# RWKV-7 mixer of a decoder trunk: the second half of a pair done for both heads at a time, with K = 64 products alternating between row groups

## The chip, the cores and the metric

The kernel runs on one core of one Trainium2 chip. The metric is the device time of one execution in microseconds, taken as the median of several runs. Engines are named as in the profile: PE (TensorE), PEld (its weight loads), DVE (VectorE), ACT (ScalarE), POOL (GpSimd), SP (SyncE, which issues the DMAs).

## The reference

Two decoder layers work on 512 tokens of width 1024. Each layer normalizes x, projects it by one matrix w_in, runs four token mixers (MLA, HGRN2, S5, RWKV-7) on slices of the projection, merges them with gates, and then does cross attention and a gated FFN. The change is inside RWKV-7, which has 8 heads of 64 channels. Per head and token:

```
def step(st, inp):
    r_t, k_t, v_t, w_t, kk_t, a_t = inp
    sa = jnp.einsum('bhvk,bhk->bhv', st, -kk_t)
    st = (st * w_t[:, :, None, :] + sa[..., None] * (kk_t * a_t)[:, :, None, :]
          + v_t[..., None] * k_t[:, :, None, :])
    return st, jnp.einsum('bhvk,bhk->bhv', st, r_t)
```

## The kernel before, in words

Dense products (`dense`, lines 331 to 333) stand for nearly all of the kernel. Each 128x128 block of weights is split in two fp32r parts, and three 128x512 products a block are added up in a bank of tag mm.

RWKV is computed in chunks of 128 tokens, four of them. `rwkv_pair` handles two heads at a time: head 0 lies on partitions 0 to 63, head 1 on 64 to 127. There are four pairs a layer, eight in all. A pair has a front half on bank tag st (one bank): elementwise work that makes al, be, kt and rt, then the product be x al for each head (line 908, K = 64), masked into rab by a predicated copy (line 909), then the inverse of a triangular matrix by 31 short steps on DVE (lines 924 and 926) and small products. The back half uses bank tag rw (two banks, handed out in turn, so that a new one waits for the one two before it to be released) and tag rwy (one bank). It transposes al, be, kt and v (line 993). Then a loop over the two heads does the rest, head 0 first: three masked K = 64 products (line 1016, copies at 1017), gak x v (1020), U (1024), the output and state matrices RY and PQ (1035, 1036), and then four steps over the chunks, in each of which a y product (1047) goes into the bank of tag rwy and a state product (1050, 64 columns) is scaled by DVE (1051) for the next step. Behind the loop come the normalization of y, a transpose, and a gating product (1083) whose bank is the last one of tag rw in the pair.

In grb and grk each chunk has 256 columns: 64 for head 0, 128 for the head in hand (the masked product, written anew for each head), 64 for head 1. All these products are f32; each stands in the trace as two matmuls.

The order of the instructions on each engine is made when the program is built. A scheduler takes instructions by priority and by its own estimate of when operands and banks are free. Pairs have their place in the order of the input projections (`mixers`, `in_order`), and dense products of those projections are put in where a pair has to wait. At run time each engine takes its instructions in that order.

Of the kernel before, what the change touches and what calls it, by code (L numbers as in the profile page):

```python
# [9 lines left out]
F32 = mybir.dt.float32  # L10
# [4 lines left out]
ALU = mybir.AluOpType  # L15
# [5 lines left out]
S = 512  # L21
MEM = 256
P = 128
# [77 lines left out]
UPPER, UPPER_EQ, HGM = 0, 1, 2  # L101
# [151 lines left out]
class Trunk:  # L253
# [62 lines left out]
    def bank(self, tag="mm", bufs=None):  # L316
        bufs = BANKS[tag]
        return self.ps.tile([P, 512], F32, tag=tag, name=tag, bufs=bufs)
# [470 lines left out]
    def rwkv_consts(self, pool):  # L789

        nc = self.nc
        z = lambda n, shape: pool.tile(shape, F32, name=n)
        self.gak = z("rgak", [P, 4, P])
        self.grb, self.grk = (z(n, [P, 4, 2 * P]) for n in ("rgrb", "rgrk"))
        self.rab = z("rab", [P, 2, 4, P])
        self.rmt = z("rmt", [P, 8, P])
        self.rm64 = z("rm64", [P, 8, 64])
        self.rvz = [z(f"rvz{h}", [P, 4, P]) for h in range(2)]
        self.rsi = [[z(f"rsi{h}{i}", [P, 64]) for i in range(4)] for h in range(2)]
        for t in [self.gak, self.grb, self.grk, self.rmt, self.rm64] + self.rvz:  # L800
            nc.gpsimd.memset(t, 0.0)
        nc.vector.tensor_copy(self.rab, self.ident.unsqueeze(1).unsqueeze(1).to_broadcast([P, 2, 4, P]))
        for h in range(2):
            for t in self.rsi[h]:
                nc.vector.tensor_copy(t, self.kcm(f"eye_k{1 - h}"))
# [20 lines left out]
    def rwkv_pair(self, l, j, pool, hv):  # L826

        nc = self.nc
        V, G, AC, PE = nc.vector, nc.gpsimd, nc.scalar, nc.tensor
        vj = lambda n: self.v(l, n, j)  # L830
        hj = lambda n: self.half(l, n, j)
        tl = lambda n, shape=None, bufs=1: pool.tile(shape or [P, S], F32, tag=n, name=n, bufs=bufs)
        c3 = lambda t: t.rearrange("p (c f) -> p c f", c=4)
        w = lambda n, shape=None: pool.tile(shape or [P, S], F32, tag="rfront", name=n, bufs=2)
        bank = lambda: self.bank("st")
# [12 lines left out]
        if l:  # L848
            vf = w("rvf")
            self.dma(vf, self.r_d[0][2, j])  # L850
            ps = bank()
# [7 lines left out]
        ps = bank()  # L859
# [5 lines left out]
        ps = bank()  # L865
# [13 lines left out]
        ff = tl("rff", [P, 3], 2)  # L879
# [12 lines left out]
        ps = bank()  # L892
        for c in range(4):
            PE.matmul(ps[:, c * P:(c + 1) * P], rb[:, 2 * c:2 * c + 2].rearrange("p h f -> p (h f)"), self.ident,
                      start=True, stop=True)
        kk = w("rkk")
        V.scalar_tensor_tensor(out=kk, in0=k, scalar=vj("k_k"), in1=ps, op0=ALU.mult, op1=ALU.mult)
        al, be, kt, rt = tl("ral", bufs=NB), tl("rbe", bufs=NB), tl("rkt"), tl("rrt")
# [1 line left out]
        V.scalar_tensor_tensor(out=be, in0=a, scalar=1.0, in1=kk, op0=ALU.add, op1=ALU.mult)  # L900
        V.scalar_tensor_tensor(out=be, in0=be, scalar=-0.5, in1=e2, op0=ALU.mult, op1=ALU.mult)

        for h in range(2):
            r0 = slice(64 * h, 64 * h + 64)
            ps = bank()
            for c in range(4):
                cs = slice(c * P, (c + 1) * P)
                PE.matmul(ps[:, cs], be[r0, cs], al[r0, cs], start=True, stop=True)
            V.copy_predicated(out=self.rab[:, h], mask=self.mask(UPPER), data=c3(ps))
        dg = tl("rdg", [P, 32, 8, 4])  # L910
        rab8 = self.rab.rearrange("p h c t -> p (h c) t")
        for q in range(4):
# [9 lines left out]
        for t in range(1, 32):  # L922
            n = t // 4 + 1
            V.tensor_tensor(out=tmp[:, :n, :t + 1], in0=M[:, :t + 1, :n].rearrange("p s c -> p c s"),  # L924
                            in1=E[:, t, :t + 1].unsqueeze(1).to_broadcast([P, n, t + 1]), op=ALU.mult)
# [15 lines left out]
        ps = bank()  # L941
# [9 lines left out]
        ps = bank()  # L951
# [10 lines left out]
        ps = bank()  # L962
# [4 lines left out]
        ps = bank()  # L967
# [13 lines left out]
        bon = tl("rbon", [P, 8], 2)  # L981
        V.tensor_copy(bon, st[:, 0:8])

        w = lambda n, shape=None: pool.tile(shape or [P, S], F32, tag="rback", name=n, bufs=3)
        bank = lambda: self.bank("rw")
        rh2 = tl("rrh", [P, 2, 4, P])
        rh = [rh2[:, h] for h in range(2)]
        gak, grb, grk = self.gak, self.grb, self.grk

        def tposed(src):  # L990
            ps = bank()
            for c in range(4):
                PE.transpose(ps[:, c * P:(c + 1) * P], src[:, c * P:(c + 1) * P], self.ident)
            return c3(ps)

        ps = tposed(al)
# [1 line left out]
            hs = slice(64 * h, 64 * h + 64)  # L998
            AC.copy(out=rh[h][:, :, hs], in_=ps[:, :, hs])
        for gt, x in ((grb, be), (grk, kt)):  # L1000
            AC.copy(out=gt.rearrange("p c (b f) -> p c b f", b=4)[:, :, 0::3],
                    in_=tposed(x).rearrange("p c (b f) -> p c b f", b=2))
        ps = tposed(v)
        for h in range(2):
            AC.copy(out=self.rvz[h][:, :, 64 - 64 * h:P - 64 * h], in_=ps[:, :, 64 * h:64 * h + 64])
        py = self.bank("rwy")
        for h in range(2):
            r0 = slice(64 * h, 64 * h + 64)
            vs = slice(64 - 64 * h, P - 64 * h)
            vz = self.rvz[h]  # L1010
            for gt, x, y, m in ((gak, kt, al, UPPER), (grb[:, :, 64:192], be, rt, UPPER_EQ),
                                (grk[:, :, 64:192], kt, rt, UPPER_EQ)):
                ps = bank()
                for c in range(4):
                    cs = slice(c * P, (c + 1) * P)
                    PE.matmul(ps[:, cs], x[r0, cs], y[r0, cs], start=True, stop=True)  # L1016
                V.copy_predicated(out=gt, mask=self.mask(m), data=c3(ps))
            ps = bank()
            for c in range(4):
                PE.matmul(ps[:, c * 64:c * 64 + 64], gak[:, c], vz[:, c, vs], start=True, stop=True)  # L1020
            AC.copy(out=rh[h][:, :, vs], in_=ps[:, :256].rearrange("p (c f) -> p c f", c=4))
            ps = bank()
            for c in range(4):
                PE.matmul(ps[:, c * P:(c + 1) * P], MT[:, 4 * h + c], rh[h][:, c], start=True, stop=True)
            U = w("rU", [P, 4, P])
            AC.copy(out=U, in_=c3(ps))
            RY = w("rRY")
            PQ = tl("rPQ", [P, 3, 64], 2)
            yo, po = (64, 0) if h == 0 else (0, 128)
            for b in range(2):  # L1030
                ps = bank()
                for c in range(2 * b, 2 * b + 2):
                    g, o = ((64 * h, 64 * h + 192), 0) if c < 3 else ((64, 192), yo)
                    out = ps[:, 192 * (c % 2) + o:192 * (c % 2) + o + g[1] - g[0]]
                    PE.matmul(out, U[:, c], grb[:, c, g[0]:g[1]], start=True, stop=False)  # L1035
                    PE.matmul(out, vz[:, c], grk[:, c, g[0]:g[1]], start=False, stop=True)
                p3 = ps[:, :384].rearrange("p (c f) -> p c f", c=2)
                y = lambda t: c3(t)[:, 2 * b:2 * b + 2]
                V.tensor_tensor(out=y(RY)[r0], in0=p3[r0, :, yo:yo + P], in1=y(rt)[r0], op=ALU.add)
                AC.copy(out=y(RY)[vs], in_=p3[vs, :, yo:yo + P])  # L1040
                n = 2 - b
                V.tensor_tensor(out=PQ[:, 2 * b:2 * b + n], in0=p3[:, :n, po:po + 64],
                                in1=self.kcm(f"eye_k{h}").unsqueeze(1).to_broadcast([P, n, 64]), op=ALU.add)
            V.memset(self.rsi[h][0][r0], 0.0)
            for c in range(4):
                si = self.rsi[h][c]
                PE.matmul(py[:, c * P + 64 * h:c * P + 64 * h + 64], RY[:, c * P:(c + 1) * P], si, start=True, stop=True)
                if c < 3:
                    ps = bank()
                    PE.matmul(ps[r0, :64], PQ[:, c], si, start=True, stop=True)  # L1050
                    V.tensor_scalar(out=self.rsi[h][c + 1][r0], in0=ps[r0, :64], scalar1=ff[r0, c:c + 1], scalar2=None,
                                    op0=ALU.mult)

        y8 = py.rearrange("p (g f) -> p g f", g=8)
        mu = tl("rmu", [P, 8])
# [12 lines left out]
                        in1=lnw.unsqueeze(1).to_broadcast([P, 4, P]), op=ALU.mult)  # L1068
        b4 = bon.rearrange("p (c h) -> p c h", c=4)
        y4 = y2.rearrange("p (c h) f -> p c h f", c=4)  # L1070
        for h in range(2):
            vs = slice(64 - 64 * h, P - 64 * h)
            nc.vector.tensor_tensor(out=y4[:, :, h], in0=self.rvz[h][:, :, vs], in1=b4[:, :, h:h + 1].to_broadcast([P, 4, 64]),
                            op=ALU.mult)
        nc.vector.tensor_tensor(out=yc, in0=yc, in1=y2, op=ALU.add)
        ps = bank()
# [3 lines left out]
        ps = bank()  # L1080
# [557 lines left out]
```

## Time and profile before

| what | us |
|---|---|
| three runs | 2773.11, 2774.59, 2781.51 |
| median | 2774.59 |
| profiled execution | 2776.61 |
| its span | 2774.5 |
| PE busy in it | 2714.2 (98%) |
| DVE busy in it | 1816.6 (65%) |
| ACT busy in it | 1112.5 (40%) |

The mean granted clock of TensorE is 0.991. The span runs from the first to the last instruction. Busy times of matmuls overlap and their ends are modelled, so distances between starts tell more than lengths. Slices and windows show when an engine is busy, and the rows in order of time show what is beside what.

### The profile page before, as it was taken

How to read it: one execution, taken by the hardware profiler on the slowest of the kernel's cores; microseconds unless marked ns; L12 is line 12 of the kernel's file. 1: busy time of each engine (PE TensorE's matmuls, PEld its weight loads, DVE VectorE, ACT ScalarE, POOL GpSimd, SP SyncE). 2: the span in 40 equal slices, each digit the busy share in tenths (PEclk: the TensorE clock that was granted, in tenths of full speed). 3: DMA queues.
4: the chain of work that ended last, by engine and by line, in shares of the span. 5: the costliest groups of instructions: out<-in, count | busy, mean ns of one | idle time of the engine just before them, and what ended most of it. 6: DMA issues, size and time to landing. Idle time of an engine off the chain costs nothing.

```text
span 2774.5 us, 37768 instructions
## 1 busy us (share of the span) xinstructions
PE 2714.2 (98%) x14176; PEld 2211.9 (80%) x14176; DVE 1816.6 (65%) x3784; ACT 1112.5 (40%) x1766; POOL 46.5 (2%) x155
## 2 busy tenths in 40 slices
PE   7999999999999999999999999999999999999997
PEld 6878877877788888888888878778777888888886
DVE  6678789675576566546466787797655855664563
ACT  5333343345554443223243333443565534432232
POOL 1000000000000000000000000000000000000000
PEclk9999999999999999999999999999999999999999
DMA  6322233233673233333343232333437632233332
GB/s 196 96 74 71 72 104 103 95 126 110 224 247 120 84 99 97 95 97 99 125 134 99 74 94 63 108 100 98 131 112 254 211 106 77 92 99 98 92 99 76
DMA packets 134534, 315.71 MB, mean 114 GB/s; under 512 B 18384, under 2 KB 38480, under 8 KB 134352
## 3 DMA queue, kind: packets, MB, share of 16 engines
q1 hardware_dynamic: 134352, 313.31, 36.2%
q8 instruction: 112, 1.84, 0.3%
q14 instruction: 70, 0.57, 0.1%
HBM read 266.32 MB, written 45.61 MB: 112 GB/s over the span
## 4 chain that ended last, share of the span: by engine, by line
PE 64%; DVE 5%; DMA 1%; issue 1%; ACT 1%; SPq 0%; DVEq 0%; POOL 0%; ACTq 0%
PE mm L332 17%; PE mm L331 17%; PE mm L333 17%; DVE wlo L239 1%; PE rwy L659 1%; PE hg L1372 1%; PE rw L659 1%; PE mm L354 1%; PE mm L355 1%; PE rw L1520 1%; PE mm L353 1%; PE rw L1016 1%; DVE rdg L924 1%; DVE rdg L926 0%; PE rw L1035 0%
## 5 line engine op out<-in xcount | busy, mean ns | idle before, releaser
L331 PE MATMUL mm<-hh,whi 128*128 128x512 f32 x2144 | 851.2, 397 | 3.1 <-ACT wa L473 2.4
L332 PE MATMUL mm<-hl,whi 128*128 128x512 f32 x2144 | 851.0, 397 | 0.1
L333 PE MATMUL mm<-hh,wlo 128*128 128x512 f32 x2144 | 849.5, 397 | 0.0
L238 ACT ACTIVATE whi<-raw 128x1024 fp32r<-128x1024 f32 (+1 forms) x404 | 418.6, 1037 | 740.5 <-PE mm L332 607.8
L239 DVE TENSOR_TENSOR wlo<-raw,whi 128x1024 fp32r<-128x1024 f32 (+1 forms) x404 | 482.8, 1195 | 294.8 <-ACT whi L238 285.6
L331 PEld LDWEIGHTS mm<-hh,whi 128*128 128x128 f32 x2144 | 404.9, 189 | 88.8 <-ACT wa L473 2.9
L332 PEld LDWEIGHTS mm<-hl,whi 128*128 128x128 f32 x2144 | 405.1, 189 | 85.8 <-issue 4.7
L333 PEld LDWEIGHTS mm<-hh,wlo 128*128 128x128 f32 x2144 | 405.4, 189 | 82.3 <-issue 2.3
L331 PE MATMUL mm<-ah,whi 128*128 128x512 f32 x352 | 136.9, 389 | 0.0
L332 PE MATMUL mm<-al,whi 128*128 128x512 f32 x352 | 136.9, 389 | 0.0
L333 PE MATMUL mm<-ah,wlo 128*128 128x512 f32 x352 | 136.9, 389 | 0.0
L588 DVE TENSOR_TENSOR x<-mm,x 128x512 f32<-128x512 f32 x64 | 44.2, 690 | 123.1 <-PE mm L333 123.1
L331 PE MATMUL mm<-oh,whi 128*128 128x512 f32 x256 | 99.9, 390 | 1.6 <-ACT g L559 1.1
L333 PE MATMUL mm<-oh,wlo 128*128 128x512 f32 x256 | 99.6, 389 | 0.0
L332 PE MATMUL mm<-ol,whi 128*128 128x512 f32 x256 | 99.6, 389 | 0.0
L711 DVE TENSOR_TENSOR gt<-mm,rstd 128x512 f32<-128x512 f32 x44 | 30.5, 692 | 98.2 <-PE mm L333 94.3
L924 DVE TENSOR_TENSOR rdg<-rdg,rE 128x2 f32<-128x2 f32 (+30 forms) x248 | 84.0, 339 | 3.5
L718 ACT ACTIVATE cv<-cv 128x512 f32<-128x512 f32 x44 | 27.8, 632 | 129.7 <-DVE cv L716 129.7
L333 PEld LDWEIGHTS mm<-ah,wlo 128*128 128x128 f32 x352 | 66.1, 188 | 13.7
L331 PEld LDWEIGHTS mm<-ah,whi 128*128 128x128 f32 x352 | 66.1, 188 | 13.7
L332 PEld LDWEIGHTS mm<-al,whi 128*128 128x128 f32 x352 | 66.1, 188 | 13.7
L721 DVE TENSOR_TENSOR up<-mm,rstd 128x512 f32<-128x512 f32 x44 | 30.4, 692 | 63.9 <-PE mm L333 63.9
(511 smaller groups left out, 4158.0 us busy)
## 6 DMA issues: line engine op xcount, KB each, us to landing
raw<-w SPq DMA_DIRECT2D x384, 512.0 KB, 3.6
g_d<-g SPq DMA_DIRECT2D x64, 256.0 KB, 2.1
gin<-g_d SPq DMA_DIRECT2D x64, 256.0 KB, 3.7
oin<-o_d SPq DMA_DIRECT2D x32, 256.0 KB, 3.6
mt<-memT SPq DMA_DIRECT2D x32, 128.0 KB, 3.4
x<-xT SPq DMA_DIRECT2D x16, 256.0 KB, 5.6
raw<-wm SPq DMA_DIRECT2D x12, 256.0 KB, 2.9
xk_d<-xkt SPq DMA_DIRECT2D x16, 128.0 KB, 2.5
```

The costliest lines, as they stand in the source:

```text
L238: nc.scalar.activation(out=self.hi, in_=raw, func=AF.Copy)
L239: nc.vector.tensor_tensor(out=self.lo, in0=raw, in1=self.hi.bitcast(F32), op=ALU.subtract)
L331: nc.tensor.matmul(ps[:, :N], hi, xh, start=i == 0, stop=False)
L332: nc.tensor.matmul(ps[:, :N], hi, xl, start=False, stop=False)
L333: nc.tensor.matmul(ps[:, :N], lo, xh, start=False, stop=i == n - 1)
L353: nc.tensor.matmul(o, xh[:, ts], wh, start=first, stop=False)
L588: self.nc.vector.tensor_tensor(out=self.x[n], in0=ps, in1=self.x[n], op=ALU.add)
L659: nc.tensor.matmul(out, x, y, start=first and n == 0, stop=last and n == 2)
L711: nc.vector.tensor_tensor(out=gt[:, 2:], in0=ps, in1=rs, op=ALU.mult)
L718: nc.scalar.activation(out=cv, in_=cv, func=AF.Silu)
L721: nc.vector.tensor_tensor(out=up, in0=ps, in1=rs, op=ALU.mult)
L924: V.tensor_tensor(out=tmp[:, :n, :t + 1], in0=M[:, :t + 1, :n].rearrange("p s c -> p c s"), in1=E[:, t, :t + 1].unsqueeze(1).to_broadcast( ...
```

## The change

A function `products` makes one kind of K = 64 product for both heads. It takes two banks of tag rw, and for each chunk it writes the product of head 0 into one and that of head 1 into the other; the two predicated copies follow. The front product be x al uses it too, and so moves from tag st to tag rw. The loop over the heads is taken apart: gak x v of both heads goes into one bank; then U of both; then RY and PQ, by halves of the chunks, head after head; then three state steps, each with the state products of both heads into the two partition halves of one bank; then all eight y products. So that both heads can be kept at once, grb and grk have 384 columns a chunk, gak two tiles, and the tag rback four buffers instead of three.

```diff
-        self.gak = z("rgak", [P, 4, P])
-        self.grb, self.grk = (z(n, [P, 4, 2 * P]) for n in ("rgrb", "rgrk"))
+        self.gak = [z(f"rgak{h}", [P, 4, P]) for h in range(2)]
+        self.grb, self.grk = (z(n, [P, 4, 3 * P]) for n in ("rgrb", "rgrk"))
...
-        for h in range(2):
-            r0 = slice(64 * h, 64 * h + 64)
-            ps = bank()
+        rows = [slice(64 * h, 64 * h + 64) for h in range(2)]
+
+        def products(x, y, gts, m):
+
+            ps = [self.bank("rw") for _ in range(2)]
             for c in range(4):
                 cs = slice(c * P, (c + 1) * P)
-                PE.matmul(ps[:, cs], be[r0, cs], al[r0, cs], start=True, stop=True)
-            V.copy_predicated(out=self.rab[:, h], mask=self.mask(UPPER), data=c3(ps))
+                for h in range(2):
+                    PE.matmul(ps[h][:, cs], x[rows[h], cs], y[rows[h], cs], start=True, stop=True)
+            for h in range(2):
+                V.copy_predicated(out=gts[h], mask=self.mask(m), data=c3(ps[h]))
+
+        products(be, al, [self.rab[:, h] for h in range(2)], UPPER)
...
-        w = lambda n, shape=None: pool.tile(shape or [P, S], F32, tag="rback", name=n, bufs=3)
+        w = lambda n, shape=None: pool.tile(shape or [P, S], F32, tag="rback", name=n, bufs=4)
...
+        products(kt, al, gak, UPPER)
+        ps = bank()
         for h in range(2):
...
+                PE.matmul(ps[:, 256 * h + c * 64:256 * h + c * 64 + 64], gak[h][:, c], self.rvz[h][:, c, vs[h]],
+                          start=True, stop=True)
+        for h in range(2):
+            AC.copy(out=rh[h][:, :, vs[h]], in_=ps[:, 256 * h:256 * h + 256].rearrange("p (c f) -> p c f", c=4))
+        products(be, rt, [grb[:, :, m] for m in mid], UPPER_EQ)
+        products(kt, rt, [grk[:, :, m] for m in mid], UPPER_EQ)
...
+        for b in range(2):
+            for h in range(2):
...
+        for c in range(3):
+            ps = bank()
+            for h in range(2):
+                PE.matmul(ps[rows[h], :64], PQ[h][:, c], self.rsi[h][c], start=True, stop=True)
+            for h in range(2):
+                V.tensor_scalar(out=self.rsi[h][c + 1][rows[h]], in0=ps[rows[h], :64], scalar1=ff[rows[h], c:c + 1],
+                                scalar2=None, op0=ALU.mult)
+        py = self.bank("rwy")
+        for h in range(2):
             for c in range(4):
-                si = self.rsi[h][c]
...
+                PE.matmul(py[:, c * P + 64 * h:c * P + 64 * h + 64], RY[h][:, c * P:(c + 1) * P], self.rsi[h][c],
+                          start=True, stop=True)
```

## Rows read from the trace of the kernel before

**Rows 1.** The page, parts 1 and 2: busy times, and busy tenths in 40 slices.

```profile
PE 2714.2 (98%) x14176; PEld 2211.9 (80%) x14176; DVE 1816.6 (65%) x3784; ACT 1112.5 (40%) x1766; POOL 46.5 (2%) x155
...
PE   7999999999999999999999999999999999999997
```

**Rows 2.** Busy time by stretch; columns PE, PEld, DVE, ACT, POOL, clock, DMA.

```profile
100.00:550.00 450.00, 440.65 (x2788) 355.78 (x2788) 353.99 (x978) 173.28 (x301) 11.12 (x33) 0.99 0.29 88
```

**Rows 3.** Order of time, PE: first and last K = 64 runs; start, length, operation.

```profile
129.16 0.40 PE L332 MATMUL mm<-hl,whi 128*128 128x512 f32 x1
129.39 0.39 PE L333 MATMUL mm<-hh,wlo 128*128 128x512 f32 x1
129.71 1.16 PE L908 MATMUL st<-ral,rbe 64*128 64x128 f32 x8
...
1897.75 1.16 PE L1016 MATMUL rw<-ral,rkt 64*128 64x128 f32 x8
1898.83 0.49 PE L332 MATMUL mm<-hl,whi 128*128 128x512 f32 x1
1899.16 0.33 PE L1047 MATMUL rwy<-rsi,rRY 128*128 128x64 f32 x2
1899.42 1.16 PE L1016 MATMUL rw<-rrt,rbe 64*128 64x128 f32 x8
1900.42 1.05 PE L1016 MATMUL rw<-rrt,rkt 64*128 64x128 f32 x8
1901.40 0.77 PE L1020 MATMUL rw<-rvz,rgak 128*128 128x64 f32 x5
```

**Rows 4.** Groups by line and shape: one kind of K = 64 product; busy, idle before.

```profile
L1016 PE MATMUL rw<-rrt,rkt 64*128 64x128 f32 x128 | 18.0, 280 | 0.3 <-DVE rgak L1017 0.3
```

**Rows 5.** Order of time, PE: two heads of two pairs side by side.

```profile
1605.82 0.60 PE L1016 MATMUL rw<-rrt,rkt 64*128 64x128 f32 x3
1606.15 0.37 PE L908 MATMUL st<-ral,rbe 64*128 64x128 f32 x1
1606.26 0.27 PE L1016 MATMUL rw<-rrt,rkt 64*128 64x128 f32 x1
1606.37 0.27 PE L908 MATMUL st<-ral,rbe 64*128 64x128 f32 x1
1606.37 0.27 PE L1016 MATMUL rw<-rrt,rkt 64*128 64x128 f32 x1
...
1607.24 0.43 PE L1020 MATMUL rw<-rvz,rgak 128*128 128x64 f32 x2
```

**Rows 6.** Order of time, PE: a state step of head 0 in the first pair.

```profile
203.79 0.39 PE L333 MATMUL mm<-hh,wlo 128*128 128x512 f32 x1
204.02 0.33 PE L1047 MATMUL rwy<-rsi,rRY 128*128 128x64 f32 x2
204.28 0.33 PE L1050 MATMUL rw<-rsi,rPQ 128*64 128x64 f32 x2
204.54 0.50 PE L331 MATMUL mm<-hh,whi 128*128 128x512 f32 x1
204.87 0.39 PE L332 MATMUL mm<-hl,whi 128*128 128x512 f32 x1
```

**Rows 7.** Order of time: second pair's front product, and the first pair's end.

```profile
217.30 1.16 PE L908 MATMUL st<-ral,rbe 64*128 64x128 f32 x8
218.39 1.10 PE L1020 MATMUL rw<-rvz,rgak 128*128 128x64 f32 x8
219.30 0.37 PE L354 MATMUL mm<-wlo,hh 128*128 128x256 f32 x1
...
235.94 0.33 PE L1047 MATMUL rwy<-rsi,rRY 128*128 128x64 f32 x2
...
251.25 0.76 DVE L1083 SCALAR_TENSOR_TENSOR rgg<-rw,vec,rgg 128x512 f32<-128x512 f32 x1
```

**Rows 8.** Groups by line and shape, DVE: one kind of predicated copy.

```profile
L1017 DVE COPY_PREDICATED rgrk<-masks,rw 128x512 f32<-128x512 uint8 x16 | 11.7, 729 | 0.9 <-PE rw L1016 0.8
```

More of the change, by code (lines that the diff above doesn't have):

```diff
@@ L799, in rwkv_consts @@
         self.rsi = [[z(f"rsi{h}{i}", [P, 64]) for i in range(4)] for h in range(2)]
-        for t in [self.gak, self.grb, self.grk, self.rmt, self.rm64] + self.rvz:
+        for t in self.gak + [self.grb, self.grk, self.rmt, self.rm64] + self.rvz:
             nc.gpsimd.memset(t, 0.0)
@@ L1000, in rwkv_pair @@
         for gt, x in ((grb, be), (grk, kt)):
-            AC.copy(out=gt.rearrange("p c (b f) -> p c b f", b=4)[:, :, 0::3],
+            AC.copy(out=gt.rearrange("p c (b f) -> p c b f", b=6)[:, :, 0::5],
                     in_=tposed(x).rearrange("p c (b f) -> p c b f", b=2))
@@ L1005, in rwkv_pair @@
             AC.copy(out=self.rvz[h][:, :, 64 - 64 * h:P - 64 * h], in_=ps[:, :, 64 * h:64 * h + 64])
-        py = self.bank("rwy")
+        vs = [slice(64 - 64 * h, P - 64 * h) for h in range(2)]
+        mid = [slice(64 + P * h, 64 + P * h + P) for h in range(2)]
+        products(kt, al, gak, UPPER)
+        ps = bank()
         for h in range(2):
[L1008 to L1018, printed above, removed]
-            for c in range(4):
-                PE.matmul(ps[:, c * 64:c * 64 + 64], gak[:, c], vz[:, c, vs], start=True, stop=True)
-            AC.copy(out=rh[h][:, :, vs], in_=ps[:, :256].rearrange("p (c f) -> p c f", c=4))
+            for c in range(4):
+                PE.matmul(ps[:, 256 * h + c * 64:256 * h + c * 64 + 64], gak[h][:, c], self.rvz[h][:, c, vs[h]],
[4 more added lines that the diff above has]
+        products(kt, rt, [grk[:, :, m] for m in mid], UPPER_EQ)
+        U, RY, PQ = [], [], []
+        for h in range(2):
             ps = bank()
@@ L1024, in rwkv_pair @@
                 PE.matmul(ps[:, c * P:(c + 1) * P], MT[:, 4 * h + c], rh[h][:, c], start=True, stop=True)
[L1025 to L1030, printed above, removed]
+            U.append(w("rU", [P, 4, P]))
+            AC.copy(out=U[h], in_=c3(ps))
+        for h in range(2):
+            RY.append(w("rRY"))
+            PQ.append(tl("rPQ", [P, 3, 64], 2))
+            V.memset(self.rsi[h][0][rows[h]], 0.0)
@@ L1031, in rwkv_pair @@
+        for b in range(2):
+            for h in range(2):
+                r0 = rows[h]
+                yo, po = (64, 0) if h == 0 else (0, 128)
                 ps = bank()
                 for c in range(2 * b, 2 * b + 2):
[L1033 to L1036, printed above, removed]
+                    g = slice(192 * h, 192 * h + 192) if c < 3 else mid[h]
+                    o = 192 * (c % 2) + (0 if c < 3 else yo)
+                    out = ps[:, o:o + g.stop - g.start]
+                    PE.matmul(out, U[h][:, c], grb[:, c, g], start=True, stop=False)
+                    PE.matmul(out, self.rvz[h][:, c], grk[:, c, g], start=False, stop=True)
@@ L1037, in rwkv_pair @@
                 p3 = ps[:, :384].rearrange("p (c f) -> p c f", c=2)
                 y = lambda t: c3(t)[:, 2 * b:2 * b + 2]
-                V.tensor_tensor(out=y(RY)[r0], in0=p3[r0, :, yo:yo + P], in1=y(rt)[r0], op=ALU.add)
-                AC.copy(out=y(RY)[vs], in_=p3[vs, :, yo:yo + P])
+                V.tensor_tensor(out=y(RY[h])[r0], in0=p3[r0, :, yo:yo + P], in1=y(rt)[r0], op=ALU.add)
+                AC.copy(out=y(RY[h])[vs[h]], in_=p3[vs[h], :, yo:yo + P])
                 n = 2 - b
-                V.tensor_tensor(out=PQ[:, 2 * b:2 * b + n], in0=p3[:, :n, po:po + 64],
+                V.tensor_tensor(out=PQ[h][:, 2 * b:2 * b + n], in0=p3[:, :n, po:po + 64],
@@ L1043, in rwkv_pair @@
                                 in1=self.kcm(f"eye_k{h}").unsqueeze(1).to_broadcast([P, n, 64]), op=ALU.add)
-            V.memset(self.rsi[h][0][r0], 0.0)
-            for c in range(4):
-                si = self.rsi[h][c]
[L1047 to L1052, printed above, removed]
+        for c in range(3):
+            ps = bank()
+            for h in range(2):
+                PE.matmul(ps[rows[h], :64], PQ[h][:, c], self.rsi[h][c], start=True, stop=True)
+            for h in range(2):
+                V.tensor_scalar(out=self.rsi[h][c + 1][rows[h]], in0=ps[rows[h], :64], scalar1=ff[rows[h], c:c + 1],
+                                scalar2=None, op0=ALU.mult)
@@ L1054, in rwkv_pair @@
+        py = self.bank("rwy")
+        for h in range(2):
+            for c in range(4):
+                PE.matmul(py[:, c * P + 64 * h:c * P + 64 * h + 64], RY[h][:, c * P:(c + 1) * P], self.rsi[h][c],
+                          start=True, stop=True)
         y8 = py.rearrange("p (g f) -> p g f", g=8)
```

## The prediction, made before the changed kernel was built or timed

> **What bounds the kernel now.** I read the page's busy shares first, then busy time by stretch, then the groups by line, and last the order in time. TensorE is busy in 2714.2 of the 2774.5 us of the span [rows 1]. The RWKV pairs run in two stretches, about 100 to 550 us for the first layer and 1500 to 1950 us for the second. In the first TensorE is busy 440.65 of 450 us, with 0.99 of the clock granted, and VectorE 353.99 [rows 2]. So the limit is TensorE's own issue of work. The pairs are background work between dense products of w_in, which are ready to fill any gap. What the change is worth is therefore the TensorE time it frees, less what new waits take back.
>
> The lengths of matmuls in the groups are modelled and overlap, so I price by distance between starts. A dense 128x512 product starts 0.23 us after the one before (129.16 to 129.39) [rows 3].
>
> An f32 product stands in the trace as two matmuls. Each kind of K = 64 product has 128 matmuls (8 pairs x 2 heads x 4 chunks x 2) [rows 4]; the four kinds (L908 once, L1016 three times) make 512. In the run of 16 that begins at 1899.42 the sixteen take until 1901.40, 1.98 us. The first and the last stretch are longer by some 0.1 us each, which leaves 0.112 us for one, however little of the array it uses [rows 3]. The price beside that is at the edges. The step into such a run is 0.32 (129.39 to 129.71) against 0.23; a run of 8 takes 1.08 (1897.75 to 1898.83) against 8 x 0.112 = 0.90; and the dense product behind it holds 0.33 against 0.23 [rows 3]. That is 0.09 + 0.18 + 0.10 = 0.37 us a run. In order of time the 512 stand in 61 unbroken runs, of which rows 3 hold the first and the last.
>
> Now: 512 x 0.112 + 61 x 0.37 = 57.3 + 22.6 = 79.9 us.
>
> **The change, part by part.**
>
> *K = 64 products of both heads alternate.* Head 0 reads partitions 0 to 63 and head 1 partitions 64 to 127, into two banks. The kernel before never writes them so, but once the scheduler put them side by side: L1016 of one head and L908 of the other, in different banks, from 1605.82. There the two start within the same hundredth of a microsecond, each at its own pace of 0.11 us, and all 16 are through at 1607.24: 1.42 us, where the serial run took 1.98 [rows 3, 5]. So two row groups do run at once. The one doubt is the order. An f32 product is two matmuls, so the new order is two of head 0, two of head 1; in rows 5 the heads mix one by one at the start times, whatever the order in the queue was. Bounds for a product of both heads: 1.98 us if nothing overlaps, 16 x 0.112 / 2 plus 0.3 of edges = 1.20 if all does. I take 1.42, the measured one, which contains a short hiccup and lies nearer the full overlap. 31 of the 32 products are not overlapped yet: 31 x 0.56 = 17 us saved (bounds 0 and 24).
>
> *Fewer edges.* 32 products of both heads instead of 64 of one. At best 32 runs. The scheduler cuts some (as now) and can no longer join two kinds in one run, since each takes both banks; I take 36. (61 - 36) x 0.37 = 9 us saved (bounds 4 with 50 runs, 11 with 32).
>
> *State products in runs of their own.* Now a state step is a y product (L1047) and a state product (L1050, 64 columns). From the dense start at 203.79 to the one at 204.87 is 1.08 us with two dense products in it [rows 6], so a step costs 1.08 - 2 x 0.23 = 0.62. 48 of these and 16 lone y products at about 0.25 (0.26 from 204.02 to 204.28) make 34 us. Afterwards there are 24 steps of two state products in opposite column groups, without the y product: 0.62 - 0.11 for the y matmuls, and the second state product adds between 0 (fully beside the first) and 0.22 (behind it). I take 0.15: 24 x 0.66 = 16. The 16 y matmuls of a pair become one run; the nearest shape, 128x64 with full weights, takes 0.91 us for 8 (218.39 to 219.30) [rows 7], so 8 x 1.82 = 15. Sum 31: 3 us saved, with 1 and 7 as bounds.
>
> Page "TensorEngine Tiling (Array Packing)" of the Trainium skill, section "Performance Considerations", says a matmul carries some 60 cycles of overhead on TRN2 and that no tiling factor should be taken from a dimension that is already small. By that the second state product would cost its full 0.22, and the sum would be 2 us smaller; no row here shows the pair.
>
> *gak times v, U, Y.* Same matmuls. gak x v of both heads is one run instead of two: 1 us at most from fewer handovers between full-speed and f32 products; I take 1. VectorE and ScalarE keep the same instructions with the same sizes (8 predicated copies a pair of about 0.73 us [rows 8], the same rh, U, RY and PQ copies). The larger grb, grk and gak cost SBUF space and longer zero fills on GpSimd once a layer, far ahead of the first product at 129.71 us [rows 3], so 0. No DMA is added, and SP's queue is passed by nothing new.
>
> *New waits.* Each product now takes both rw banks, and what follows in that tag waits for two predicated copies, 2 x 0.73 = 1.46 us, and on VectorE these queue behind whatever is there. TensorE runs in order, so a wait that the scheduler misjudges holds the dense products behind it. Nothing is lost where dense products are put in between; without any cover it is 32 x 1.46 = 47 us. Today the products behind such a copy show 0.3 us of idle time for all eight pairs [rows 4], the nearest row; with both banks taken I take 3.
>
> The front product (be x al) moves from the single st bank to the two rw banks. In the second pair it starts at 217.30, while the first pair's back half lasts until the gating product, which starts at 251.25 on VectorE and frees its last rw bank [rows 7]. That overlap of 34 us goes, because tiles of a tag rotate. In return head 1 no longer comes after head 0. Its last y product stood at 235.94, some 15 us ahead of the gating product [rows 7]; now it would stand a few us behind head 0's steps, which pass 204.87 in rows 6, near 210. So the last bank is free near 225, and the next front product begins some 8 us later than now. Per layer that is about 3 x 8 us of chain against about 30 us gained at the last pair. TensorE is at nine tenths or more in every slice behind the pairs as well [rows 1], so nothing waits for their end, and I cost it at 0.
>
> **Sum.** 17 + 9 + 3 + 1 - 3 = 27 us from the measured prices, up to 24 + 11 + 7 + 1 = 43 us at the other end. The measured 1.42 contains a hiccup that a regular order need not have, so I place the forecast a little above the first figure: 31 us. The profiled execution took 2776.61 us, 2.0 above the median of 2774.59, and gives 2745.6; against the median the forecast is **2743.5 us**. Its own range is 2728 to 2757.
>
> **Rivals.**
>
> *A. No overlap in the new order.* The second matmul of each f32 product blocks the queue, and the heads run one after the other. Left are the edges, 9, state 3, gak 1, less 3: 10 us, 2764.5. For it: no row shows two-by-two order with certainty. Against: in rows 5 the groups keep their own pace whichever comes first.
>
> *B. Saved TensorE time turns into waiting.* VectorE is busy 79% in such a stretch [rows 2]; with 16 us less of TensorE work in each it would be at 354 of 434, 82%, and chains through its long solve show up as gaps. If half the gain goes: 2759. For it: the share. Against: TensorE idles under 10 us of 450 now [rows 2].
>
> *C. Slower: exposed copies.* The two banks are filled together and emptied one after the other, and the next product of the chain stands in TensorE's queue with no dense product before it. Exposed at the full 1.46 us this takes 47 us against the 34 gained without the 3 for waits: 2787.5. It decides from 34 / 32 = 1.06 us a product. For it: rw has only two banks, so nothing of the tag can go ahead. Against: dense products can stand in between, and three of them (0.69 us) cover half; the row that shows this wait has 0.3 us of it [rows 4]. The Trainium skill says as much on its page "TensorEngine Tiling (Array Packing)", section "Performance Considerations": tiling makes TensorE faster but not the emptying of PSUM, which may become the limit.
>
> **How the numbers follow.** Forecast 0.60, A 0.12, B 0.18, C 0.06, 0.04 for no change out of shifts in the schedule. What this kernel can be told apart by is 0.3%, 8.3 us; its bounds are 2766.3 and 2782.9. A lies just inside the faster side of that edge, so half of it counts as same. Faster: 0.60 + 0.18 + 0.06 = 0.84; same 0.06 + 0.04 = 0.10; slower 0.06. The range reaches from 2728 to A at 2767; outside are C and the most favourable end.
>
> **What would show it.** In order of time, L-rows of the new products as one run of 16 matmuls of both heads, 1.2 to 1.45 us from first start to the next operation, near 32 to 40 runs in all; 24 short runs of state products at 0.5 to 0.7 us net; TensorE's idle time in the two stretches still about 10 us each; the front product of the next pair right after the gating product of the pair before. Runs of nearly 2 us mean A; idle time before products released by predicated copies means C; a VectorE above 85% with gaps on TensorE means B. The forecast is wrong if the sixteen take over 1.7 us or the stretches wait more than 10 us longer.

## The result: slower, and the profile after

The changed kernel took 2802.7 us (median of five), the kernel before 2773.1 us beside it. Four of the five executions lie between 2789.2 and 2803.6 us; the fifth took 6450.9 us and is left out, as a slow one, of the ratio on record, 1.0079 [1.0058, 1.0100]. The forecast was 2743.5 us, with a range of 2728 to 2767 and a chance of 0.06 for slower: wrong in sign. The profiled execution took 2789.17 us with a span of 2787.4. It is the fastest of its kernel; the three next to it ran at a lower mean clock (0.976 to 0.978 against 0.981).

The page, parts 1 and 2; then the first layer's pairs as one stretch (columns as in [rows 2]):

```profile
PE 2724.8 (98%) x14176; PEld 2216.4 (80%) x14176; DVE 1832.1 (66%) x3784; ACT 1106.9 (40%) x1762; POOL 49.6 (2%) x157
...
PEclk9999999999999999999999999789999999999998
```

```profile
100.00:550.00 450.00, 436.50 (x2769) 350.76 (x2769) 358.50 (x963) 171.76 (x299) 10.58 (x32) 0.98 0.29 89
```

Against [rows 1] TensorE is busy 11 us longer, though it has the same 14176 matmuls and less to do for the pairs. Its idle time over the whole span is 62.6 us, 60.3 before; in the stretch of [rows 2] it idles 13.5 us of the 450, 9.4 before. So nearly all of the longer span is time in which TensorE counts as busy. The clock row shows a 7 and an 8 just behind 1740 us, and an 8 at the very end, where it had only nines before.

**K = 64 products, now L911.** In order of time on TensorE, two unbroken runs of sixteen matmuls:

```profile
123.12 1.16 PE L911 MATMUL rw<-ral,rbe 64*128 64x128 f32 x16
124.21 0.50 PE L333 MATMUL mm<-hh,wlo 128*128 128x512 f32 x1
...
357.39 1.96 PE L911 MATMUL rw<-rrt,rbe 64*128 64x128 f32 x16
359.37 2.06 PE L911 MATMUL rw<-rrt,rkt 64*128 64x128 f32 x16
361.35 0.50 PE L332 MATMUL mm<-hl,whi 128*128 128x512 f32 x1
```

The first run is the change as written: 1.09 us to the next start, with starts in pairs of 7 ns and then 105 ns. That is the time of a run of eight, 1.08 [rows 3]: the second head is free. The second run is the same code at the price of the serial run, 1.98 us. Its starts are mostly 112 ns apart, as if one head's eight matmuls stood ahead of the other's (the rows do not name the head). Of the 256 places where two matmuls could start within 30 ns, 44 do (5 before). The runs number 55 (61 before; 36 foreseen), and all 512 matmuls hold 64.2 us from start to next start, against 69.2.

**State products, now L1056.** A step of both heads, in order of time, and the next operation:

```profile
208.16 0.34 PE L1056 MATMUL rw<-rsi,rPQ 128*64 128x64 f32 x4
208.43 0.50 PE L333 MATMUL mm<-hh,wlo 128*128 128x512 f32 x1
```

Four matmuls take 0.27 us, two took 0.26 [rows 6]. State and y products together hold 21.5 us from start to next start (7.9 and 13.6); they held 28.3 (12.2 and 16.2).

**The front product of the next pair.** VectorE's and then TensorE's order of time:

```profile
210.53 0.68 DVE L901 SCALAR_TENSOR_TENSOR rbe<-rbe,re 128x512 f32<-128x512 f32 x1
246.50 0.74 DVE L1095 SCALAR_TENSOR_TENSOR rgg<-rw,vec,rgg 128x512 f32<-128x512 f32 x1
```

```profile
238.47 0.93 PE L911 MATMUL rw<-ral,rbe 64*128 64x128 f32 x6
240.19 0.48 PE L911 MATMUL rw<-ral,rbe 64*128 64x128 f32 x2
...
242.70 0.71 PE L911 MATMUL rw<-ral,rbe 64*128 64x128 f32 x4
```

Its operand is written at 210.53, 5 us earlier than before, but the product starts at 238.47, 21 us later than the 217.30 of [rows 7]. It stands in line for the two rw banks behind the previous pair's last tiles. The four chunks of each head now lie in four pieces, none alternating. The gating product of the last pair starts where it did in layer 1 (553.5 against 553.9 us), and some 42 us later in layer 2 (1984 against 1943).

**The end of the solve.** TensorE's waits for VectorE's last solve step, first before the change, then after (total, times, longest):

```profile
PE st L949 <- DVE rdg L930: 7.2, 7, 2.6
```

```profile
PE st L955 <- DVE rdg L936: 13.9, 5, 3.4
```

What follows such a wait is seen in the second layer's third pair: order of time on TensorE, then busy time by stretch (PE, PEld, DVE, ACT, POOL, granted clock, DMA share, GB/s):

```profile
1778.34 0.39 PE L331 MATMUL mm<-hh,whi 128*128 128x512 f32 x1
1778.57 0.39 PE L332 MATMUL mm<-hl,whi 128*128 128x512 f32 x1
1781.52 0.97 PE L955 MATMUL st<-rdg,rab 32*32 32x32 f32 x16 [2.57 <-DVE rdg L936]
...
1783.02 0.63 PE L331 MATMUL mm<-hh,whi 128*128 128x512 f32 x1
1783.45 0.63 PE L332 MATMUL mm<-hl,whi 128*128 128x512 f32 x1
```

```profile
1750.00:1760.00 10.00, 9.38 (x46) 6.84 (x44) 9.87 (x25) 4.02 (x7) 0.00 (x0) 1.00 0.55 165
...
1770.00:1780.00 10.00, 8.95 (x40) 7.09 (x38) 9.72 (x20) 4.83 (x7) 0.00 (x0) 1.00 0.34 114
1780.00:1790.00 10.00, 8.48 (x60) 5.85 (x60) 2.32 (x6) 3.45 (x8) 0.00 (x0) 0.58 0.24 75
...
1800.00:1810.00 10.00, 10.00 (x41) 7.46 (x40) 0.57 (x2) 2.55 (x3) 0.00 (x0) 0.50 0.00 0
...
1830.00:1840.00 10.00, 9.73 (x55) 7.97 (x55) 8.70 (x27) 4.47 (x8) 1.87 (x5) 1.00 0.40 134
```

TensorE reaches the step behind the solve before VectorE is done and stands 2.57 us, and then the granted clock is 0.50 from 1781.7 to 1826.1 us. Dense products come 0.43 us apart instead of 0.23; TensorE counts as fully busy. In this trace there are six waits of 1.3 us or more at the end of a solve (the row above has five; one of 1.39 us is put down to another VectorE step), and at each of the six the clock drops to its lower level (1.2 of 2.4 GHz), for 3.4 to 44 us. Before there was one such wait (2.56 us at 378.7), with 6.8 us behind it.

VectorE is nearly full ahead of this wait (9.87 and 9.72 of 10 us), but that does not tell the two kernels apart. The 30 us ahead of the end of the second pair's solve, before the change (wait 1.04 us) and after it (3.24 us), same columns:

```profile
239.50:269.50 30.00, 28.84 (x162) 23.22 (x161) 29.23 (x95) 12.62 (x22) 0.63 (x2) 1.00 0.26 82
```

```profile
252.40:282.40 30.00, 26.74 (x140) 22.11 (x139) 27.08 (x69) 9.24 (x14) 0.29 (x3) 1.00 0.38 114
```

Over the eight solves VectorE is busy 27.6 to 29.5 of the last 30 us before, 27.1 to 29.0 after, and a solve takes 35 to 62 us before, 30 to 47 after. So from the second pair of a layer on the solves start later, since their product starts later, but they are not slower. Why TensorE's order puts the step behind a solve too early by more than before is not shown.

**The account.** Outside the last 20 us the clock is at half for 88.7 us, against 37.5 before. A microsecond at half costs at most half a microsecond, so 51 us more cost up to 26. In two executions of one and the same program (below) 43 us more at half cost 15 us, 0.36 each; by that it is 18. TensorE's own saving is 5 (K = 64) and 7 (state and y), 12 us; its idle time grew by 2, and the products gak x v and U take 3 more at full clock. So an estimate of 11 to 19 us slower comes out. The profiled executions differ by 2789.17 - 2776.61 = 12.6 us.

The other executions can be estimated in the same way. The clock has two levels here, 1 and 0.5, so a mean clock of c means that 2 (1 - c) of the span was at half. Over the 19 executions of that one program a straight line gives 0.41 us for each us at half. The four executions near 2800 us have a median clock of 0.977, the kernel before 0.991: 78 us more at half, 32 us, less 12, plus 2 and 3, is 25 us. The medians lie 27 us apart without the one of 6450.9 us.

### The profile page after: what moved, and what is told of

Read it like the earlier page. It is cut to its first block, busy times and chain, and to the rows that moved or that the text cites. A ratio compares the mean times of both kernels' runs of the same rounds, so it can differ in the third digit from the quotient of the medians.

```text
span 2787.4 us, 37765 instructions
## 1 busy us (share of the span) xinstructions
PE 2724.8 (98%) x14176; PEld 2216.4 (80%) x14176; DVE 1832.1 (66%) x3784; ACT 1106.9 (40%) x1762; POOL 49.6 (2%) x157
## 4 chain that ended last, share of the span: by engine, by line
PE 84%; DVE 11%; ACT 2%; issue 1%; DMA 1%; SPq 0%; DVEq 0%; POOL 0%; ACTq 0%; POOLq 0%
PE mm L332 20%; PE mm L333 20%; PE mm L331 20%; DVE wlo L239 2%; PE rw L911 2%; DVE rdg L930 2%; PE hg L1384 2%; PE rw L1532 1%; DVE rdg L932 1%; PE mm L354 1%; PE mm L355 1%; PE mm L353 1%; PE rw L659 1%; ACT whi L238 1%; PE rwy L659 1%
## 5 line engine op out<-in xcount | busy, mean ns | idle before, releaser
L332 PEld LDWEIGHTS mm<-al,whi 128*128 128x128 f32 x352 | 66.1, 188 | 13.7
L331 PEld LDWEIGHTS mm<-ah,whi 128*128 128x128 f32 x352 | 66.1, 188 | 13.6
```

Source lines behind the costliest of these rows:

```text
L331: nc.tensor.matmul(ps[:, :N], hi, xh, start=i == 0, stop=False)
L332: nc.tensor.matmul(ps[:, :N], hi, xl, start=False, stop=False)
```

## Experiments

Theory: the loss comes from the front product's move to the tag rw. The pairs hardly overlap any more, the solve ends against a crowded VectorE, TensorE waits and its clock falls. (The crowded VectorE is the link that the rows above do not bear out; the experiments test the rest.) Besides, the alternation was mostly undone by the scheduler's order. Rivals: exposed copies (rival C of the prediction), and no true overlap (rival A). Each was timed against the kernel before, at 2776 us in all three batches. Line numbers shift with each edit, and the cuts of code show its main lines.

**1. The eight products of two heads as one block that the scheduler may not split.**

```diff
-            for c in range(4):
+            with self.tc.tile_critical():
+              for c in range(4):
...
```

> The changed kernel with the eight K = 64 products of a kind made one atomic block for the scheduler, so that the heads really alternate; nothing else differs. Theory 1 (in the changed kernel the scheduler mostly issues head 0's four products before head 1's, since their bank is free first): 32 runs of 16 matmuls, K = 64 time from 64 us to about 40 us, runs from 55 to 32, so 25 to 33 us less than the changed kernel, 2765 to 2775 us, if the time at half clock stays. Rival (alternation gives nothing because the copies behind it become the wait): TensorE idles ahead of what waits for the copies by 0.5 us or more a product, and the time stays at 2790 to 2800 us.

Measured: 2967.1 us, 1.0695 [1.0679, 1.0711]. The alternation is there: 32 runs of sixteen, 244 of 256 places with two starts within 30 ns, 49.9 us in all. But TensorE now stands ahead of these blocks. Its two largest waits there:

```profile
PE rw L912 <- DMA o_d<-rgg: 19.0, 5, 4.5
PE rw L912 <- DMA rv<-r_d: 7.2, 3, 2.9
```

The products read neither. From the matmul before to the first of the block it is 73 us over 32 blocks. The longest waits of this run stand elsewhere (49.8 us in all for ScalarE's s5zs, 1.4 before), and its clock is 0.957; what holds those up was not followed further. The expectation missed, since the edit brought waits of its own; against rival A it speaks, about the theory it says little.

**2. The change with the front product back in the st bank (`bank()` at this place), head after head.**

```diff
-        products(be, al, [self.rab[:, h] for h in range(2)], UPPER)
+        for h in range(2):
+            ps = bank()
+            for c in range(4):
+                cs = slice(c * P, (c + 1) * P)
+                PE.matmul(ps[:, cs], be[rows[h], cs], al[rows[h], cs], start=True, stop=True)
+            V.copy_predicated(out=self.rab[:, h], mask=self.mask(UPPER), data=c3(ps))
```

> The changed kernel with only the front product be x al put back as it was, head after head in the single st bank. Theory 2 (the front product in tag rw has to wait for the end of the pair before, the pairs no longer overlap, their long solves are pushed into crowded stretches of VectorE, TensorE waits at the end of a solve and its clock then falls to half): front products again ahead of the pair before's gating product, time at half clock back from about 90 to about 40 us in the body, 2765 to 2780 us. Rival (the loss is from the taken-apart head loop, or chance of the schedule): 2790 us or more.

Measured: 2775.4 us (2767.2 to 2790.7), 1.0001 [0.9982, 1.0020]. Putting back this one edit takes back the whole loss, 27 us of the medians. The waits at the solve's end fall from 13.9 to 8.6 us:

```profile
PE st L960 <- DVE rdg L941: 8.6, 5, 2.7
```

K = 64 products hold 63.5 us, state and y 21.7: the alternation is as broken as in the change, and yet the loss is gone. That nothing is gained on the kernel before, with 12 us saved here too, goes with the clock: 0.987 in the median against 0.991, which at 0.41 is 9 us.

**3. Both edits.**

> Both edits: atomic alternation for the three back-half products, front product in st as before the change. Theories 1 and 2 together: 2740 to 2755 us, 20 to 33 us under the kernel before. If only theory 1 holds, about the same as the atomic run alone; if only theory 2 holds, about the same as the front-in-st run.

Measured: 2889.4 us, 1.0412 [1.0383, 1.0440]. The block's waits again; fewer blocks, less loss. It tells nothing more.

**4. The kernel before, with the front product's bank alone moved.**

```diff
-            ps = bank()
+            ps = self.bank("rw")
```

> The kernel before with one edit: its front product, head after head, takes its bank from tag rw instead of st. Theory 2: pairs stop overlapping (each front product behind the gating product of the pair before), head 1 still behind head 0 so the chain is longer than in the changed kernel by about 25 us a pair; 10 to 40 us slower than before with more time at half clock. Rival (the front product's bank does not matter): within 8 us of the kernel before.

Measured: 2793.0 us (2789.0 to 2794.3), 1.0063 [1.0050, 1.0077]. One line of the change, put into the kernel before, costs 17 us. TensorE's waits for the solve's end rise to 10.2 us, with 3.45 and 4.34 the longest, and the clock falls at both (17.1 and 13.7 us at half):

```profile
PE st L949 <- DVE rdg L930: 10.2, 4, 4.3
```

The median clock is 0.983 against 0.991, 44 us more at half; at 0.41 that is about 18 us, the whole of the loss.

**5. Experiment 2 with the alternation kept by order.** The first product of two heads waits for the last reader of the rw bank before, and each further one is placed behind the one before without a wait.

```diff
+                    mm = PE.matmul(ps[h][:, cs], x[rows[h], cs], y[rows[h], cs], start=True, stop=True)
+                    if prev is None:
+                        behind(mm, freed, mybir.DependencyClass.Sync)
+                    else:
+                        behind(mm, prev, mybir.DependencyClass.NoSync)
+                    prev = mm
...
```

> The run with the front product back in st, and in the back half the eight products of a kind kept in alternating order: the first waits until the bank before is read (so both banks are free), each further one is queued behind the last, and nothing else is waited for, unlike in the atomic block. Theory 1: K = 64 time of the back half from 46 to about 30 us, and 10 to 20 us less than the run with the front in st at the same granted clock; 2752 to 2768 us. Rival (copies become the wait): TensorE idle ahead of the later products up by 10 us or more, no gain over that run.

Measured: 2761.2 us (2751.2 to 2787.8), 0.9950 [0.9914, 0.9986]. TensorE in order of time, a pair's three products:

```profile
364.06 1.16 PE L916 MATMUL rw<-ral,rkt 64*128 64x128 f32 x16
...
370.43 1.16 PE L916 MATMUL rw<-rrt,rbe 64*128 64x128 f32 x16
...
373.78 1.16 PE L916 MATMUL rw<-rrt,rkt 64*128 64x128 f32 x16
```

Twenty of 35 runs are whole, nearly all at 1.09 us; 173 of 192 places have two starts within 30 ns. The three later kinds hold 30.8 us where experiment 2 has 46.0. So 15 us of TensorE's time come from the alternation once it is real. The fastest runs differ by as much, 2751.2 against 2767.2. At an equal clock of 0.99, by straight lines through time and clock of the executions, this program lies at 2757 us and that of experiment 2 at 2767: some 10 us arrive. Rival C would have shown here: TensorE's waits put down to these copies are 3.4 us, against 0.6 in experiment 2, far from the 47 of the rival.

**6. The change with ten dense products put into the wait.** Their result is not used. They write the st bank before the first step behind the solve, and may start after the solve's last multiplication.

```diff
+        for i in range(10):
+            mm = PE.matmul(ps, self.hh[0][:, 0:P], self.hh[0], start=True, stop=True)
+            self.tc.add_manual_dep(mm.ins, late.ins.name, ...)
```

> The changed kernel with ten junk 128x512 products (their result is not used) in front of the first TensorE step behind the 31-step solve, started by the solve's last multiply, eight times. They add 80 x 0.23 = 18 us of TensorE work, of which the waits there (15 us in the changed kernel, at most 2.3 us each) can swallow about 12. Theory 3 (the wait at the end of a solve makes the clock fall, and the half clock behind it is where the changed kernel loses): time at half clock in the body from 90 to about 40 us, 10 to 25 us faster than the changed kernel, 2775 to 2790 us. Rival (the clock falls for something else): 5 us or more slower than the changed kernel, clock as it was.

Measured: 2812.0 us, 1.0090 [1.0058, 1.0122], a miss. The wait moved in front of the filling and grew:

```profile
PE st L949 <- DVE rdg L930: 17.9, 8, 3.4
```

Behind the one of 3.44 us at 286.0 the clock was at half for 41 us. So in this execution the edit did not do what it was for. The seven executions fall in two groups: four at 2812 to 2814 us with a clock of 0.982 or 0.983, the profiled one among them, and three at 2788 to 2793 with 0.991 to 0.993.

**7. and 8. The same filling in experiment 5 and in the kernel before.**

> The run with ordered alternation and the front in st, with the same ten junk products behind each solve. Theories 1 and 3: clock at 0.99 or over and 2750 to 2762 us, steadier than without the filling. Rival: slower than the same run without the filling by the 6 to 18 us of added work.

> The kernel before with the same ten junk products behind each solve. Its waits there are 7 us in sum and only one of them is followed by half clock, so theory 3 gives little to win: 18 us of work less about 7 of waits less about 3 of clock, 2778 to 2786 us. If it gains as much as the changed kernel does, the filling works by something else.

Measured: 2776.0 us (2770.7 to 2795.2), 1.0002 [0.9985, 1.0019], and 2790.5 us, 1.0049 [1.0033, 1.0066]. In the first the clock comes to 0.995 in the profile, with 2 x 3.4 us at half between 100 us and the last 20; but the added work, 8 pairs x 10 x 0.23 = 18 us, costs more than that gives back: it is 15 us slower than experiment 5 and 5 us slower than its repeat. The waits did not vanish (11.1 us in 8), but only one of them is over 2 us. In the kernel before, which had little to win, 14 of the 18 us are lost. Both came out slower than expected, the first as its rival had it.

**9. and 10. Experiment 5 with four filling products, and once more without.**

> The ordered kernel with four filling products (f32, 128x512, into the st bank) ahead of the first step behind the solve instead of ten. Theory (what costs time is the clock that falls behind the wait at the end of the solve, and work put into that wait costs its own length where there was no wait): ten cost 18 us a run and kept the clock near 0.995; four cost 7 us and cover about 1 us of each wait of 1.5 to 3 us, so the clock comes out between, about 0.988 to 0.993, and the time near 2758 to 2768. Rival (the wait must be covered whole, half a cover changes nothing): the clock as in the ordered kernel, 0.98 to 0.99, and 7 us longer, 2768 to 2775.

> The ordered kernel once more (the pairs' later products alternating head by head, the first product of a pair back in the st bank). If it is faster than the kernel before, it comes out at 2750 to 2775 with a ratio below 0.998 again; if the first result was a draw of the clock, at the time of the kernel before, 2770 to 2780.

Measured: with four 2758.2 us (2755.6 to 2764.7), 0.9934 [0.9918, 0.9950]; without 2770.9 us (2756.1 to 2786.6), 0.9978 [0.9960, 0.9997]. Both beat the kernel before, and the first both kernels in every run. Its waits total 10.1 us, but none is longer than 1.7:

```profile
PE st L965 <- DVE rdg L946: 10.1, 7, 1.7
```

So the fall of the clock goes with long waits more than with their total. Over ten traces, all but those of experiments 1 and 3, there are 18 waits of 2 us or more at the end of a solve, and at 17 of them the clock falls, during the wait or soon behind it; the other is one of 2.71 us in experiment 6. Of 31 waits of 1 to 2 us it falls at 8. How long it stays down does not follow the wait: 34 us behind one of 2.17, 6.8 behind one of 3.36. Nor does every fall stand at such a wait: in this run the clock is at half for 13.7 us from 1764.4, with no wait over 0.7 us in the 20 us ahead. That four filling products shorten the longest wait is what the profile shows; that another schedule without them could not do so was not tried.

The repeat gives the best view of the clock. Its profiled execution took 2786.6 us, that of experiment 5 2771.3 us: the same program (in another batch, on another chip), with nearly the same waits up to 1570 us. The second layer's first pair, first in experiment 5, then in the repeat:

```profile
1570.00:1580.00 10.00, 10.00 (x94) 9.03 (x93) 3.95 (x10) 2.70 (x7) 0.00 (x0) 0.57 0.06 24
1590.00:1600.00 10.00, 10.00 (x70) 7.31 (x71) 7.44 (x20) 7.03 (x16) 0.00 (x0) 1.00 0.03 8
```

```profile
1570.00:1580.00 10.00, 10.00 (x87) 9.07 (x85) 2.70 (x8) 3.03 (x8) 0.00 (x0) 0.50 0.01 2
1590.00:1600.00 10.00, 10.00 (x46) 8.15 (x46) 2.86 (x8) 1.27 (x2) 0.00 (x0) 0.50 0.00 0
```

Half clock lasts 10.2 us in the one and 47.8 in the other, with TensorE busy throughout. Over the whole span 43.2 us more at half stand beside 15.3 us more time. The spread is not a matter of the chip alone: within experiment 5 the executions reach from 2751.2 us at a clock of 0.992 to 2787.8 at 0.977.

## Why the prediction was wrong, step by step

**The step that failed** is the front product's move: "so nothing waits for their end, and I cost it at 0". The mechanism was seen (the overlap of 34 us goes), but it was priced by the end of the chain. The move delays the front product (by 21 us in the second pair, where the prediction had 8), and with it the solve, and TensorE waits for the solve's end within the pair, in front of dense work. Experiment 4 shows the price alone, 17 us in the kernel before; experiment 2 shows the opposite edit, 27 us. The sum had no term for the granted clock. The waiting at the solve's end is 6.7 us longer (13.9 against 7.2), and all idle time of TensorE only 2 us; the rest is clock. It could have been asked: the kernel before shows 2.56 us of that wait and 6.8 us of half clock behind it.

This step is 27 of the 59 us between forecast and median. Without it (experiment 2) the change comes out level with the kernel before, not 31 us faster. The larger part of that is the next two terms, 6 of 26 us by the products' time, and about 9 us is the clock.

**Alternation, 17 us.** The size was right, the order was not foreseen. The doubt in the prediction was two-by-two against one-by-one on the engine; the scheduler was taken to keep the order of the code. The rows fit a scheduler that issues what is ready: the first bank of two comes free first, so head 0's products go ahead. Of the saving 5 us came, edges included. Where the order holds, a product of both heads takes 1.09 us, less than the 1.42 taken and even than the bound of 1.20: 15 us for 24 products, most of them whole. Experiment 5 shows it.

**Fewer edges, 9 us.** 55 runs, not 36: 6 x 0.37 = 2 us, part of the 5 above. Same cause.

**State products, 3 us (1 to 7).** The order was right and the term undersized: 7 us. The second head's state product costs 0.01 us, not 0.15. The other reading in the prediction, the full 0.22 for the second product, is not borne out: the two start 6 to 7 ns apart and the pair takes 0.27 us. The Trainium skill, "TensorEngine Tiling (Array Packing)", section "Performance Considerations", from whose warning on small dimensions that reading came, also names a stationary side of 64 as a case for two column tiles, and this trace agrees with the latter.

**gak times v, 1 us, and new waits, 3 us.** The 1 us did not come: these products hold 14.6 us against 13.4, none of it at half clock. U's products, for which the sum had no term, hold 19.2 us against 15.3; 16 of the 128 matmuls run at half clock, and without any half clock experiments 2, 7 and 9 have 16.2 to 18.3. The products behind the copies show 0.1 us of idle time for a whole kind ([rows 4] had 0.3), so the 3 us were not spent here; where the order holds, in experiment 5, the copies' waits are 3.4 us, about the term. The row of one kind in the change:

```profile
L911 PE MATMUL rw<-rrt,rkt 64*128 64x128 f32 x128 | 18.3, 290 | 0.1
```

**Rivals.** A is refuted by the runs of 1.09 us. C forecast the sign, but by another mechanism: the copies are hidden in the row above, and cost 3.4 us in experiment 5. B comes nearest: saved TensorE time turned to waiting behind VectorE. It was priced at half the gain, because it was seen as a matter of VectorE's share, 353.99 of 450 [rows 2]. That share is 358.50 now (345.15 in the second layer, 356.16 before), and VectorE is no fuller ahead of the solves' ends than it was. So the share is not what made the waits longer, and B lacked the clock behind them.

**What stays open.** Why TensorE waits longer for solves that are no slower; why the clock came back after 10 us in one execution and after 48 in another of the same program; and whether experiment 6 is slower than the change at all: the medians lie 9 us apart, but the ratios, 1.0090 [1.0058, 1.0122] and 1.0079 [1.0058, 1.0100], do not tell them apart.

## What to carry to other kernels

Moving a tile to another tag is a change of order, not of place: ask which work of the next stage starts in front of which of this one, and which engine it then meets. Products that must alternate have to be ordered as such, since this scheduler broke them up where their banks came free one after the other; a block that may not be split cost far more here than it saved (experiment 1). And a wait of TensorE is not worth its own length alone: look at the granted clock behind it.

## What was not expected of the hardware

Two K = 64 f32 products on opposite halves of the rows run wholly beside each other when they alternate: 16 matmuls in 1.09 us, 8 in 1.08. Two 64-column products likewise: 0.27 us against 0.26. And the clock stays at its lower level for 34 to 48 us at times, with TensorE busy 10.00 of 10 us; one and the same program took from 2751 to 2788 us in 19 runs, and time and mean clock go together in them: its two profiled executions had mean clocks of 0.985 and 0.977 at 2771.3 and 2786.6 us.
